# State-space layer of an S5 / sparse-attention decoder: two weight conversions held until the scan ends, the sample group's outputs held until the last states, filler matrix products put behind two steps of the scan

## The chip, the cores and the metric

One core of one Trainium2 chip runs the whole program. The metric is the device time of one execution in microseconds (us); the lower the better. The traces shown are those of one execution taken by the hardware profiler.

## What is computed

Two layers of a decoder run for a prompt group (512 positions) and a sample group (8 sequences of one position each); the weights are shared. The change lies in the first mixer of layer 0, a state-space layer (S5):

```python
x_re = einsum('blgc,gpc->blgp', ug, bb_re)      # inputs into 64 groups of 64 complex states
x_im = einsum('blgc,gpc->blgp', ug, bb_im)
...
_, _, h_re, h_im = lax.associative_scan(complex_affine_combine, (a_re, a_im, x_re, x_im), axis=1)
y = (einsum('blgp,gcp->blgc', h_re, c_re) - einsum('blgp,gcp->blgc', h_im, c_im)) + d_skip * u32
g = gelu(y)
a, b = split(g @ w_glu, 2, axis=-1)
out = a * sigmoid(b)
```

After it come a dense SwiGLU layer, sparse attention, and a mixture of experts, none of which the change touches.

## The kernel before, in words

`build` makes the program; it calls `s5` first, then the GLU loop (lines 283 to 292), the SwiGLU, attention and experts. `s5` cuts the 512 positions into 64 blocks of 8. Its stages are these.

- **Chunks** (lines 565 to 597). For each of eight chunks of eight groups, in the order 0, 4, 1, 5, 2, 6, 3, 7: VectorE (DVE) builds Pm, TensorE (PE) transposes it (L575), ScalarE (ACT) copies the result to Wi (L576), DVE adds a part to `dsk` (L578), PE multiplies Wi with the inputs U (L586), and ACT copies the block sums into the state array XS (L589, four copies a chunk). GpSimd (POOL) builds the output weights Em (L537 to L539) and, in between, the powers Ar, Ai of the transition (L546 to L556).
- **Scan** (lines 611 to 650). `step` does one level of a work-efficient scan over the 64 blocks: products L632 and L633, sums L636 and L638; six levels up, five levels down. DVE does columns 0 to 23 of XS with Ar and Ai held in PSUM (copied there at L607, L608), POOL does columns 24 to 31 by itself (`BLK`). DVE's columns are complete after chunk 6, POOL's only after the last one, chunk 7.
- **Prefetch** (L651). `glu_w(0)` and `glu_w(1)`: each loads 1 MB of GLU weights into a staging tile `wf` (L212; two such slots), ACT makes the f16 high part `wh` (L217) and DVE the f16 rest `wl` from `wf` and `wh` (L218). The loads of blocks 2 and 3 need the staging slots again, so they start when L218 of blocks 0 and 1 are done.
- **Sample group** (lines 659 to 677). POOL computes the sample group's new states (L659 to L665); PE computes its outputs in two halves of 32 pairs of small products (L675, L676), and ACT applies GELU (L677).
- **Prompt outputs** (lines 680 to 711). `toeplitz(b)` (L689) multiplies the inputs with a banded matrix Tp, eight products for each of eight PSUM banks b. Banks for b = 5, 6 and 7 hold Ar, Ai and the scan's scratch until DVE's scan is done; b = 0 to 4 are free earlier. When the scan is done, its states are copied from XS to Hs (L698: the real parts by DVE, the imaginary parts by ACT, two copies each for DVE's columns and two for POOL's), PE adds Hs times Em into the eight banks (L707), and ACT applies GELU (L710).
- **Into the GLU** (lines 715 to 732). PE transposes Y (L719), ACT and DVE split it into f16 parts GH and GL (L725, L726), and the GLU's products begin (L231).

What sets the order: nobody writes the order of an engine's instructions by hand. A planner takes the program in source order and gives each engine, whenever it is free by the planner's own estimate, the ready instruction that stands earliest in the source. So a later instruction is slipped into an earlier sequence wherever that sequence has a gap by the estimate. On the chip each engine then runs its list strictly in that order. `add_manual_dep` adds a wait of one instruction for another, which the planner and the chip both keep.

Of the kernel before, what the change touches and what calls it, by code (L numbers as in the profile page):

```python
# [14 lines left out]
ALU = mybir.AluOpType  # L15
# [4 lines left out]
WS = 256.0  # L20
# [144 lines left out]
def build(tc, a, o, stop=None):  # L165
    nc = tc.nc
    es = ExitStack()
    with es:
        const = es.enter_context(tc.tile_pool(name="const", bufs=1))
        res = es.enter_context(tc.tile_pool(name="res", bufs=1))  # L170
# [35 lines left out]
            else:  # L206
                V.scalar_tensor_tensor(dl, src, scale, dh, op0=ALU.mult, op1=ALU.subtract)

        def wload(src, w, n, pool=wst, tags=("wh", "wl"), parts=1):

            wf = wst.tile([128, w], F32, tag="wf", name=f"wf{n}")
            nc.sync.dma_start(wf, src)  # L212
            wh = pool.tile([128, w], F16, tag=tags[0], name=f"wh{n}")
            wl = pool.tile([128, w], F16, tag=tags[1], name=f"wl{n}")
            for i in range(parts):
                c = slice(i * w // parts, (i + 1) * w // parts)
                S.activation(wh[:, c], wf[:, c], AF.Copy, scale=WS)  # L217
                V.scalar_tensor_tensor(wl[:, c], wf[:, c], WS, wh[:, c], op0=ALU.mult, op1=ALU.subtract)  # L218
            return wh.rearrange("p (k c) -> p k c", c=128), wl.rearrange("p (k c) -> p k c", c=128)

        HV = ((0, 256), (256, NT))
# [39 lines left out]
                for c0, c1 in HV:  # L261
                    S.activation(acc[1][:, c0:c1], act[:, ob, c0:c1], AF.Square)

        def glu_w(ob):
            return wload(a["w_glu"][:, 2 * ob:2 * ob + 2].rearrange("p b k c -> p (b k c)"), 2048, f"g{ob}")

        glu_first = []
        GH, GL = s5(tc, nc, a, o, PS, const, identf, res, wst, lambda: glu_first.extend((glu_w(0), glu_w(1))))
        if stop == "s5":
            nc.sync.dma_start(o["dbg_gh"], GH)  # L270
            nc.sync.dma_start(o["dbg_gl"], GL)
# [75 lines left out]
       }  # L347


def s5(tc, nc, a, o, PS, const, identf, res, wst, prefetch):  # L350
    V, S, G, T = nc.vector, nc.scalar, nc.gpsimd, nc.tensor
    with ExitStack() as es:
        p = es.enter_context(tc.tile_pool(name="s5", bufs=1))
# [211 lines left out]
        for n_, c in enumerate((0, 4, 1, 5, 2, 6, 3, 7)):  # L565
            Pm = wst.tile([128, GC, 8, 16], F32, tag="wh", name=f"Pm{c}")
            prod_v(Pm, pfr, pfs, slice(7, None, -1), 0, b0, b1, c * GC)
            Wi = wst.tile([128, GC, 128], F32, tag="wl", name=f"Wi{c}")
            ic = idc[n_ % 2]
            S.copy(ic[:, :, 128:144], cst[:, c * 8:c * 8 + 8])  # L570
            for j0, nj in ((0, 3), (3, 3), (6, 2)):
                pt = PS(5, 6, 7)
                pv = pt[:, :nj * 144].rearrange("p (g c) -> p g c", c=144)
                for j in range(nj):
                    T.matmul(pv[:, j], Pm[:, j0 + j].rearrange("p k c -> p (k c)"), ic[:, j0 + j], start=True, stop=True)  # L575
                S.copy(Wi[:, j0:j0 + nj], pv[:, :, 0:128])  # L576
                dd = dsk[:, c * 8 + j0:c * 8 + j0 + nj]
                V.tensor_tensor(dd, pv[:, :, 128:144], dd, op=ALU.add)  # L578
            gh = c // 4
            rows = slice(gh * 64, gh * 64 + 64)  # L580
            uq = U[:, c * 8:c * 8 + 8]
            V.tensor_tensor(uq, uq, std.unsqueeze(1).to_broadcast([128, 8, 72]), op=ALU.mult)
            for h in range(2):
                px = PS(5, 6, 7)
                for j in range(4):
                    T.matmul(px[:, j * 72:j * 72 + 72], Wi[:, 4 * h + j, :], U[:, c * 8 + 4 * h + j, :], start=True, stop=True)  # L586
                gp = (c % 4) * 8 + 4 * h
                for ri in range(2):
                    S.copy(XS[rows, 1:73, ri, gp:gp + 4],  # L589
                           px[ri * 64:ri * 64 + 64, :288].rearrange("p (g n) -> p n g", g=4))  # L590
            prod_g(Em[:, c * GC:(c + 1) * GC], pr, pi, slice(1, 9), cst, csw, c * GC)
            if c in (5, 7):
                gs = slice((c - 5) * 8, (c - 5) * 8 + 16)
                for i in range(8):
                    nr_ = 16 * (i + 1)
                    nc.sync.dma_start(Tp[0:nr_, i, :].rearrange("p (h g c) -> p h g c", h=2, c=16)[:, :, gs],
                                      dsk[128 - nr_:128].rearrange("p (h g) c -> p h g c", h=2)[:, :, gs])
# [9 lines left out]
        V.tensor_copy(ArP, Ar[:, :NL])  # L607
        V.tensor_copy(AiP, Ai[:, :NL])  # L608
        m2p = PS(1), PS(2)

        def step(eng, gs, tag, l, tgt0, src0, stride, n):

            w = gs.stop - gs.start
            most = 16 if eng is G else 512 // (2 * w)
            parts = [(i, min(most, n - i)) for i in range(0, n, most)]
            while parts:
                now, parts = parts[:2], parts[2:]
                ops = []
                for k, (i, m) in enumerate(now):
                    def vw(b, r):  # L620
                        b += i * stride
                        return XS[:, b:b + (m - 1) * stride + 1:stride, r, gs]
                    m1 = lt2.tile([128, 16, 2, w], F32, tag=tag, name=f"{tag}a")[:, :m]
                    if eng is G:
                        m2 = lt2.tile([128, 16, 2, w], F32, tag=tag, name=f"{tag}b")[:, :m]
                    else:
                        m2 = m2p[k][:, :m * 2 * w].rearrange("p (n r w) -> p n r w", n=m, r=2)
                    A, B = (ArP, AiP) if eng is V and l < NL else (Ar, Ai)
                    ar = A[:, l:l + 1, gs].unsqueeze(2).to_broadcast([128, m, 2, w])
                    ai = B[:, l:l + 1, :, gs].to_broadcast([128, m, 2, w])  # L630
                    tgt = vw(tgt0, slice(0, 2))
                    eng.tensor_tensor(m1, vw(src0, slice(0, 2)), ar, op=ALU.mult)  # L632
                    eng.tensor_tensor(m2, vw(src0, slice(1, None, -1)), ai, op=ALU.mult)  # L633
                    ops.append((m1, m2, tgt))
                for m1, m2, tgt in ops:
                    eng.tensor_tensor(m2, m1, m2, op=ALU.add)  # L636
                for m1, m2, tgt in ops:
                    eng.tensor_tensor(tgt, tgt, m2, op=ALU.add)  # L638


        BLK = ((V, slice(0, 24), "sv"), (G, slice(24, 32), "sg"))
        for blk in BLK:
            for l in range(6):
                d = 1 << l
                n = 64 // (2 * d)
                step(*blk, l, 2 * d, d, 2 * d, n)
            for l in range(4, -1, -1):
                d = 1 << l
                n = 64 // (2 * d) - 1
                step(*blk, l, 3 * d, 2 * d, 2 * d, n)  # L650
        prefetch()  # L651
        nc.sync.dma_start(o["s5p"].rearrange("r p g -> p r g"), XS[:, 64])

        m1 = late.tile([128, 2, 32, 8], F32, name="hm1")
# [15 lines left out]
        for half in range(2):  # L670
            py = PS(4 + half)
            for j in range(32):
                g = half * 32 + j
                c0 = j * 16
                T.matmul(py[:8, c0:c0 + 16], U[:, g, 64:72], Tp[:, 7, g * 16:g * 16 + 16], start=True, stop=False)  # L675
                T.matmul(py[:8, c0:c0 + 16], h0A[:, g, :], Em[:, g, 0, :], start=False, stop=True)  # L676
            S.activation(ys[:, half * 512:(half + 1) * 512], py[:8], AF.Gelu_apprx_tanh)  # L677

# [12 lines left out]
                             skip_group_check=True)  # L691
        for b in range(4):
            toeplitz(b)
        for (_, gs, _), bs in zip(BLK, ((0, 1, 2, 3, 4, 5), (6, 7))):
            for gh in range(2):
                for ri in range(2):
                    e = S.copy if ri else V.tensor_copy
                    e(Hs[ri * 64:ri * 64 + 64, gh * 32 + gs.start:gh * 32 + gs.stop, :],  # L698
                      XS[gh * 64:gh * 64 + 64, 0:64, ri, gs].rearrange("p n g -> p g n"))
            for b in bs:  # L700
                if b not in pys:
                    toeplitz(b)
                py = pys[b]
                for j in range(4):
                    for gh in range(2):
                        g = gh * 32 + b * 4 + j
                        T.matmul(py[gh * 64:gh * 64 + 64, j * 128:(j + 1) * 128], Hs[:, g, :],  # L707
                                 Em[:, g].rearrange("p i c -> p (i c)"), start=False, stop=(j == 3),
                                 skip_group_check=True)
                S.activation(Y[:, :, 4 * b:4 * b + 4, :].rearrange("p i g c -> p g i c"),  # L710
                             py.rearrange("p (g i c) -> p g i c", g=4, i=8), AF.Gelu_apprx_tanh)
# [1198 lines left out]
```

## Time and profile before

| | us |
|---|---|
| median of 3 runs | 1503.71 (1503.48 to 1504.97) |
| the profiled execution, whole | 1505.52 |
| its span, first instruction to last | 1503.7 |

The profile gives busy times by engine (PE matrix products, PEld their weight loads, DVE, ACT, POOL; SP issues most transfers), the chain of work that ended last, and, by query, instructions in order of time and sums by stretch. A line of the timeline has the start and the length in us, the engine, the source line, what it writes and reads, its shape, how many instructions were merged into the line, and in brackets how long the engine had stood idle and what ended that. The granted clock is given as a share of 2.4 GHz: 1.00 or 0.50 (1.2 GHz), between them for a mixed stretch. PE's instructions overlap, so their pace is read from start to start.

### The profile page before, as it was taken

To read this page: it belongs to the slowest core of one execution; us is meant where nothing else is said; L and a number is where in the kernel's file an instruction comes from. 1 tells how busy PE (TensorE), PEld (TensorE's weight loads), DVE (VectorE), ACT (ScalarE), POOL (GpSimd) and SP (SyncE) were. 2 spreads that over 40 slices of the span, in tenths; PEclk is the share of its full clock that TensorE was granted. 3 is DMA by queue.
4 is the path that set the end of the run, shared out by engine and by line. 5 is a ranking of instruction groups with operands and counts; after the bars stand their busy time and mean duration, and the time that the engine had idled before them with its cause. 6 is when DMAs were issued, how large, how long until landed. Compare 5 with 4: busy or idle time off the path is not lost.

```text
span 1503.7 us, 37358 instructions
## 1 busy us (share of the span) xinstructions
PE 1363.0 (91%) x15585; PEld 1180.1 (78%) x15585; DVE 943.2 (63%) x1641; ACT 771.2 (51%) x1421; POOL 557.4 (37%) x465
## 2 busy tenths in 40 slices
PE   4847999999999999989989979969998999999895
PEld 3836888888888888775777658837877999999884
DVE  8783566232322233594787877475766788878886
ACT  5524344232322112352787777464655776867663
POOL 4991443222222122211122323324830541734935
PEclk9977999999999999999999989968999999999997
DMA  4141742323232333352313221245989999989884
GB/s 167 60 125 58 282 169 78 113 85 112 85 113 73 116 119 139 92 163 100 121 58 99 79 65 31 65 178 199 366 265 331 347 317 380 376 293 391 315 305 147
DMA packets 82049, 262.36 MB, mean 174 GB/s; under 512 B 25242, under 2 KB 40082, under 8 KB 64338
## 3 DMA queue, kind: packets, MB, share of 16 engines
q1 hardware_dynamic: 78770, 249.24, 47.6%
q0 software_dynamic: 2816, 8.52, 1.6%
q8 instruction: 125, 2.05, 0.5%
q10 hardware_dynamic: 288, 2.14, 0.4%
q14 instruction: 50, 0.41, 0.1%
HBM read 232.30 MB, written 21.67 MB: 169 GB/s over the span
## 4 chain that ended last, share of the span: by engine, by line
PE 59%; DVE 14%; DMA 11%; ACT 5%; issue 5%; POOL 4%; SPq 2%; DVEq 0%; ACTq 0%; POOLq 0%
PE ps L231 27%; PE ps L1728 17%; DMA mf<-in_w_mo 3%; DVE ml L1578 2%; PE ps L1076 2%; DMA mf<-in_w_mi 2%; ACT mh L1577 2%; PE ps L1161 2%; DMA yr<-YS,gidxe 2%; PE ps L1676 2%; DMA st<-in_ckc 1%; PE ps L1287 1%; PE ps L1274 1%; DVE tl L205 1%; PE ps L575 1%
## 5 line engine op out<-in xcount | busy, mean ns | idle before, releaser
L1578 DVE SCALAR_TENSOR_TENSOR ml<-mf,mh 128x2048 f16<-128x2048 f32 (+1 forms) x152 | 309.3, 2037 | 77.2 <-ACT mh L1577 74.6
L1728 PEld LDWEIGHTS <-mh 128*128 128x128 f16 x4224 | 328.8, 99 | 14.2 <-ACT mh L1577 2.3
L1577 ACT ACTIVATE mh<-mf 128x2048 f16<-128x2048 f32 (+1 forms) x152 | 256.1, 1685 | 113.5 <-DMA mf<-in_w_mi 34.0
L1728 PE MATMUL ps<-XE,mh 128*128 128x64 f16 (+7 forms) x2816 | 279.9, 230 | 2.8 <-ACT mh L1577 2.1
L1728 PE MATMUL ps<-XE,ml 128*128 128x96 f16 (+7 forms) x1408 | 261.9, 230 | 4.2 <-DVE ml L1578 4.0
L1808 POOL TENSOR_TENSOR AL<-u,AH 128x272 f16<-128x272 f32 (+3 forms) x88 | 171.0, 1947 | 205.0 <-ACT AH L1807 204.0
L1728 PEld LDWEIGHTS <-ml 128*128 128x128 f16 x2112 | 205.3, 99 | 12.2 <-DVE ml L1578 5.9
L231 PEld LDWEIGHTS <-whf 128*128 128x128 f16 x1408 | 137.7, 98 | 18.4
L231 PE MATMUL ps<-GH,whf 128*128 128x256 f16 x704 | 135.7, 274 | 0.0
L231 PE MATMUL ps<-GL,whf 128*128 128x256 f16 x704 | 135.7, 274 | 0.0
L231 PE MATMUL ps<-GH,wlf 128*128 128x256 f16 x704 | 135.5, 274 | 0.0
L1728 PE MATMUL ps<-AL,mh 128*128 128x272 f16 (+7 forms) x704 | 133.7, 230 | 0.9 <-POOL AL L1808 0.9
L1728 PE MATMUL ps<-AH,mh 128*128 128x144 f16 (+7 forms) x704 | 133.1, 230 | 0.0
L1728 PE MATMUL ps<-AH,ml 128*128 128x144 f16 (+7 forms) x704 | 133.0, 229 | 0.0
L320 POOL TENSOR_TENSOR UL<-sf,UH 128x520 f16<-128x520 f32 x22 | 59.4, 2701 | 177.4 <-ACT UH L319 177.4
L317 DVE SCALAR_TENSOR_TENSOR sf<-ps,sf 128x256 f32<-128x256 f32 (+1 forms) x44 | 16.9, 424 | 140.8 <-PE ps L231 140.8
L217 ACT ACTIVATE whf<-wff 128x2048 f16<-128x2048 f32 x22 | 42.0, 1910 | 94.0 <-issue 82.0
L231 PEld LDWEIGHTS <-wlf 128*128 128x128 f16 x704 | 68.9, 98 | 9.3
L231 PEld LDWEIGHTS <-who 128*128 128x128 f16 x704 | 68.9, 98 | 9.2
L1277 DVE CUSTOM_DVE_ANT_0 st<-ps,BB 128x512 f32<-128x512 f32 (+3 forms) x128 | 61.3, 485 | 23.0 <-PE ps L1287 19.8
L1279 ACT ACTIVATE st<-st,mx 128x512 f32<-128x512 f32 (+3 forms) x128 | 71.6, 560 | 5.0 <-DVE mx L1277 4.2
L217 ACT ACTIVATE who<-wfo 128x1408 f16<-128x1408 f32 x16 | 22.0, 1377 | 91.6 <-PE ps L231 77.1
(552 smaller groups left out, 3304.5 us busy)
## 6 DMA issues: line engine op xcount, KB each, us to landing
mf<-in_w_mi SPq DMA_DIRECT2D x88, 1024.0 KB
mf<-in_w_mo SPq DMA_DIRECT2D x64, 704.0 KB
wff<-in_w_fin SPq DMA_DIRECT2D x22, 1024.0 KB
wfo<-in_w_fout SPq DMA_DIRECT2D x16, 704.0 KB
wfg<-in_w_glu SPq DMA_DIRECT2D x8, 1024.0 KB
wfq<-in_w_qk SPq DMA_DIRECT2D x8, 1024.0 KB
HS<-z SPq DMA_DIRECT2D x9, 512.0 KB
st<-in_ckc SPq DMA_DIRECT2D x16, 256.0 KB
```

What stands on the lines that cost most here:

```text
L217: S.activation(wh[:, c], wf[:, c], AF.Copy, scale=WS)
L231: T.matmul(t[:, :c1 - c0], w[:, k0 + k, :], x[k][:, c0:c1] if isinstance(x, list) else x[:, k, c0:c1], start=(first and k == 0 and wi == 0 ...
L320: G.tensor_tensor(UL[:, ob, :], sg, UH[:, ob, :], op=ALU.subtract)
L1076: T.matmul(t[:, :n], w[:, k0 + k], x[:, k, c0:c1], start=(k == 0 and i == 0), stop=(k == 7 and i == 2))
L1161: T.matmul(pv[:n], x[:, k, t0:t1], w, start=(k == 0 and i == 0), stop=(k == 7 and i == 2))
L1277: V.tensor_tensor_reduce(out=st[:, :N], in0=pS[:, :N], in1=bias_cur[0][:, r, 512 - N:], scale=1.0, scalar=3.0e38, op0=ALU.add, op1=ALU.min ...
L1279: S.activation(st[:, :N], st[:, :N], AF.Exp, bias=mx, scale=-1.0, accum_out=st8["sums"][:, 1 + br, r:r + 1])
L1577: S.activation(wh, wf, AF.Copy, scale=WS)
L1578: V.scalar_tensor_tensor(wl, wf, WS, wh, op0=ALU.mult, op1=ALU.subtract)
L1676: T.matmul(px[:, :C0 + C7], hts[tb][:n, k * 128:(k + 1) * 128], OHP[:n, tb], start=(tb == 0), stop=(tb == 4))
L1728: T.matmul(ps, w[:, k0 + k, :], x[:, k, :], start=(k == 0 and i == 0), stop=(k == kn - 1 and i == 2))
L1808: al = G.tensor_tensor(AL[r][:, ob], u, AH[r][:, ob], op=ALU.subtract)
```

## The change

The GLU's first two `wl` conversions (L218) get a wait for DVE's last scan instruction. The first product of each half of the sample group's outputs (L675) gets a wait for the last copy into XS (L589). After `toeplitz(0)` to `toeplitz(3)` in source order stand 12 and 36 new products of 128x512 f16 (the block-0 GLU weights times themselves, into PSUM bank 3, never read); the first 12 wait for DVE's scan level 2 on the way down, the other 36 for level 1. `toeplitz(4)` uses the same bank 3 and now follows them.

```diff
+        def after(x, y):
+            tc.add_manual_dep(x.ins, y.ins.name, mybir.DependencyInfo(
+                mybir.DependencyClass.Sync, mybir.DependencyReason.DATA), reason="order")
...
-                V.scalar_tensor_tensor(wl[:, c], wf[:, c], WS, wh[:, c], op0=ALU.mult, op1=ALU.subtract)
+                t = V.scalar_tensor_tensor(wl[:, c], wf[:, c], WS, wh[:, c], op0=ALU.mult, op1=ALU.subtract)
+                if y is not None:
+                    after(t, y)
...
-        GH, GL = s5(tc, nc, a, o, PS, const, identf, res, wst, lambda: glu_first.extend((glu_w(0), glu_w(1))))
+        GH, GL = s5(tc, nc, a, o, PS, const, identf, res, wst, after,
+                    lambda y: glu_first.extend((glu_w(0, y), glu_w(1, y))) or glu_first[0][0])
...
-                    S.copy(XS[rows, 1:73, ri, gp:gp + 4],
+                    fed = S.copy(XS[rows, 1:73, ri, gp:gp + 4],
...
-                    eng.tensor_tensor(tgt, tgt, m2, op=ALU.add)
+                    done[eng] = eng.tensor_tensor(tgt, tgt, m2, op=ALU.add)
...
+        steps = []
         for blk in BLK:
...
                 step(*blk, l, 3 * d, 2 * d, 2 * d, n)
-        prefetch()
+                if blk[0] is V and l in (2, 1, 0):
+                    steps.append(done[V])
+        whg = prefetch(done[V])
...
-                T.matmul(py[:8, c0:c0 + 16], U[:, g, 64:72], Tp[:, 7, g * 16:g * 16 + 16], start=True, stop=False)
+                t = T.matmul(py[:8, c0:c0 + 16], U[:, g, 64:72], Tp[:, 7, g * 16:g * 16 + 16], start=True, stop=False)
+                if j == 0:
+                    after(t, fed)
...
         for b in range(4):
             toeplitz(b)
+
+        for y, m in zip(steps[:2], (12, 36)):
+            fill = PS(3)
+            for i in range(m):
+                t = T.matmul(fill, whg[:, 4 + i % 4], whg.rearrange("p k c -> p (k c)")[:, 0:512], start=True, stop=True)
+                if i == 0:
+                    after(t, y)
```

## Rows read from the trace of the kernel before

**Rows 1.** The chain that ended last, in order of time: start, length, what.

```profile
77.89 2.63 POOL hm L660
...
85.78 2.78 POOL sga L632
...
125.85 5.34 PE ps L707 x87
```

**Rows 2.** Sums by stretch: PE, PEld, DVE, ACT, POOL busy; granted clock; DMA share; GB/s.

```profile
104.00:118.00 14.00, 0.00 (x0) 0.00 (x0) 12.09 (x26) 0.73 (x1) 11.90 (x25) 0.50 0.02 2
118.00:124.00 6.00, 5.24 (x49) 5.24 (x50) 5.03 (x8) 5.25 (x4) 0.00 (x0) 0.54 0.00 0
124.00:134.00 10.00, 8.21 (x130) 7.73 (x128) 0.00 (x0) 3.37 (x5) 0.00 (x0) 1.00 0.01 2
...
140.00:144.00 4.00, 4.00 (x24) 3.04 (x25) 1.97 (x5) 0.57 (x2) 1.81 (x1) 0.50 0.77 263
```

**Rows 3.** Timeline of POOL around the start of the scan.

```profile
77.22 0.67 POOL L659 TENSOR_TENSOR hm<-h0B,pr 128x256 f32<-128x256 f32 x1
77.80 2.72 POOL L660 TENSOR_TENSOR hm<-h0B,pr 128x256 f32<-128x256 f32 x1
...
81.67 0.63 POOL L556 TENSOR_SCALAR Ai<-Ai 128x160 f32<-128x160 f32 x1
...
85.78 2.78 POOL L632 TENSOR_TENSOR sga<-XS,Ar 128x256 f32<-128x256 f32 x1 [0.45 <-ACT XS L589]
```

**Rows 4.** Timeline of DVE: conversions, ends of scan levels, copies to Hs.

```profile
77.57 2.47 DVE L218 SCALAR_TENSOR_TENSOR wlg<-wfg,whg 128x2048 f16<-128x2048 f32 x1 [1.82 <-ACT whg L217]
...
82.34 0.50 DVE L608 COPY ps<-Ai 128x320 f32<-128x320 f32 x1 [2.09 <-POOL Ai L556]
...
85.70 2.28 DVE L218 SCALAR_TENSOR_TENSOR wlg<-wfg,whg 128x2048 f16<-128x2048 f32 x1
...
105.62 0.50 DVE L638 TENSOR_TENSOR XS<-XS,ps 128x336 f32<-128x336 f32 x1
...
108.81 0.96 DVE L638 TENSOR_TENSOR XS<-XS,ps 128x480 f32<-128x480 f32 x2
...
117.27 1.20 DVE L698 COPY Hs<-XS 64x512 f32<-64x512 f32 x2 [1.74 <-POOL XS L638]
...
119.31 0.77 DVE L638 TENSOR_TENSOR XS<-XS,ps 128x480 f32<-128x480 f32 x2
120.11 3.01 DVE L698 COPY Hs<-XS 64x1536 f32<-64x1536 f32 x2
```

**Rows 5.** Timeline of ACT: second GLU block, last copies to XS, Hs, GELU.

```profile
82.95 1.91 ACT L217 ACTIVATE whg<-wfg 128x2048 f16<-128x2048 f32 x1 [3.27 <-DMA wfg<-in_w_glu]
84.89 0.81 ACT L589 COPY XS<-ps 64x288 f32<-64x288 f32 x2
...
120.11 5.68 ACT L698 COPY Hs<-XS 64x1536 f32<-64x1536 f32 x2 [0.71 <-DVE XS L638]
132.43 4.03 ACT L710 ACTIVATE Y<-ps 128x512 f32<-128x512 f32 x8 [6.63 <-PE ps L689]
```

**Rows 6.** Timeline of PE: sample group, banded products, output products, first GLU products.

```profile
69.72 0.21 PE L675 MATMUL ps<-Tp,U 128*8 128x16 f32 x2
69.78 0.20 PE L676 MATMUL ps<-Em,h0A 128*8 128x16 f32 x2
...
79.73 1.09 PE L689 MATMUL ps<-Tp,U 128*64 128x128 f32 x16 [0.89 <-ACT XS L589]
...
118.77 3.68 PE L689 MATMUL ps<-Tp,U 128*64 128x128 f32 x32 [20.47 <-DVE ps L633]
...
132.18 1.09 PE L707 MATMUL ps<-Em,Hs 128*64 128x128 f32 x13
...
143.54 0.42 PE L231 MATMUL ps<-GH,whg 128*128 128x256 f16 x1
143.75 0.42 PE L231 MATMUL ps<-GL,whg 128*128 128x256 f16 x1
```

More of the change, by code (lines that the diff above doesn't have):

```diff
@@ L207, in hilo, with wload @@
                 V.scalar_tensor_tensor(dl, src, scale, dh, op0=ALU.mult, op1=ALU.subtract)
-        def wload(src, w, n, pool=wst, tags=("wh", "wl"), parts=1):
+        def after(x, y):
+            tc.add_manual_dep(x.ins, y.ins.name, mybir.DependencyInfo(
+                mybir.DependencyClass.Sync, mybir.DependencyReason.DATA), reason="order")
+        def wload(src, w, n, pool=wst, tags=("wh", "wl"), parts=1, y=None):
             wf = wst.tile([128, w], F32, tag="wf", name=f"wf{n}")
@@ L262, in squares, with glu_w @@
                     S.activation(acc[1][:, c0:c1], act[:, ob, c0:c1], AF.Square)
-        def glu_w(ob):
-            return wload(a["w_glu"][:, 2 * ob:2 * ob + 2].rearrange("p b k c -> p (b k c)"), 2048, f"g{ob}")
+        def glu_w(ob, y=None):
+            return wload(a["w_glu"][:, 2 * ob:2 * ob + 2].rearrange("p b k c -> p (b k c)"), 2048, f"g{ob}", y=y)
         glu_first = []
-        GH, GL = s5(tc, nc, a, o, PS, const, identf, res, wst, lambda: glu_first.extend((glu_w(0), glu_w(1))))
+        GH, GL = s5(tc, nc, a, o, PS, const, identf, res, wst, after,
+                    lambda y: glu_first.extend((glu_w(0, y), glu_w(1, y))) or glu_first[0][0])
         if stop == "s5":
@@ L347, with s5 @@
        }
-def s5(tc, nc, a, o, PS, const, identf, res, wst, prefetch):
+def s5(tc, nc, a, o, PS, const, identf, res, wst, after, prefetch):
     V, S, G, T = nc.vector, nc.scalar, nc.gpsimd, nc.tensor
@@ L609, in s5 @@
         m2p = PS(1), PS(2)
+        done = {}
         def step(eng, gs, tag, l, tgt0, src0, stride, n):
```

## The prediction

> **What bounds the kernel now.** I read the chain that ended last first, to see where the changed stage lies on it, then the timelines of the engines it passes through, then the sums by stretch for TensorE's clock. The chain goes through the changed stage on one thread only: POOL's work before the scan, the scan, ACT's copies to Hs, PE's output products [rows 1]. What is saved at the last output product is therefore saved at the end, unless the planner orders a later stage anew. PE is full behind this stage but idle in it: no matmul at all from 104 to 118 us, with the granted clock at 0.50 [rows 2].
>
> Four things in the timelines carry the argument.
> - DVE's scan cannot start before POOL's L556 (81.67 + 0.63 = 82.30), which gives Ai; DVE waits 2.09 us for it [rows 3, 4]. Ahead of L556, L660 took 2.72 us where L659 of the same shape took 0.67 [rows 3]. It ran while DVE's first conversion ran (77.57 to 80.04) [rows 4].
> - The second conversion lies inside the scan: 85.70, 2.28 us [rows 4]. POOL's first scan instruction beside it took 2.78 us [rows 3].
> - In DVE's tail stand the copies of POOL's columns: a wait of 1.74 us for POOL and 1.20 us of copying, before the scan's last level is finished at 119.31 + 0.77 = 120.08 [rows 4].
> - Then DVE copies for 3.01 us and ACT for 5.68 us, to 125.79; PE starts the mass of the output products at 125.85 and ends them at 132.18 + 1.09 = 133.27, which is 7.42 us [rows 1, 4, 5, 6].
>
> **Conversions: what their removal gives.**
> 1. The first one is gone when POOL does L660, so that one should take L659's time: 2.72 - 0.67 = 2.05 us earlier for L556, for L608 and for DVE's scan. The bound below is 0, if L660's length has another reason; I take the whole, since the overlap with the conversion is nearly exact [rows 3, 4].
> 2. The second one leaves the scan: 2.28 us.
> 3. The tail. In source order the copies of DVE's own columns come first; POOL's were slipped in ahead because POOL's columns were ready, by the planner's estimate, shortly before DVE's. DVE's end moves forward by 2.05 + 2.28 = 4.33 us. POOL's moves by the 2.1 us that L632 loses (2.78 to 0.67) and by what its start gains: it waits for the last copy into XS, which stands on ACT behind a conversion that waits 3.27 us for its load [rows 3, 5]. That copy's product on PE needs a DVE instruction that stood behind the first conversion, so it is ready about two us earlier, and the planner should then put the copy ahead of ACT's conversion. DVE thus gains more on the planner's clock than POOL does, and I take it that nothing is slipped in: 1.74 + 1.20 = 2.94 us gone. Bounds: 0 and 2.94.
>
> DVE's scan then ends at 120.08 - 2.05 - 2.28 - 2.94 = 112.8.
>
> **Conversions: what they cost in the new place.** The wait ends with DVE's last scan instruction, exactly when DVE's copies to Hs become ready, and the conversions stand earlier in the source. So I expect DVE to run both first: 2.47 + 2.28 = 4.75 us, to 117.55, with its copies (3.01) behind them, to 120.6. ACT copies from 112.8 to 118.5 [rows 4, 5]. So ACT's copies, which came last before, are replaced by DVE's: the gate for the output products is 120.6 instead of 125.8, **5.2 us** earlier. The bounds: if DVE's copies go ahead of the conversions, the gate is ACT's 118.5 (7.3 us); with nothing gained in the tail it is 123.5 (2.3 us).
>
> Behind the conversions also wait the loads of GLU blocks 2 and 3, since they need the staging slots; SP issues them at about 115 and 118 rather than before the scan. The products of the first GLU blocks are still running at 143.54 [rows 6], so these loads have over 20 us: no cost. SP's next entries are outputs and loads that wait for the scan anyway.
>
> **Sample group.** Its 256 records of products run at two per 0.06 us [rows 6], 7.7 us in all, now behind the last copy into XS, together with banded products of four banks (1.09 us each [rows 6], 4.4 us). Even from 85.7, where that copy ends now [rows 5], this is done by 97.8. PE has nothing else until the fillers, so it costs nothing; with the cover gone it would delay the fillers, which are needed by nobody. What it gives is that the last chunk's products are not cut into; that is part of item 3.
>
> **Fillers.** No row has a 512-column f16 product. The 256-column ones start 0.21 us apart at the 0.50 clock [rows 2, 6], so I estimate 0.42 us at 1.2 GHz and half of that, 0.21, at 2.4. Scan level 2 ends at 105.62 + 0.50 = 106.12 now [rows 4] and, 4.33 earlier, at 101.8; level 1 at 108.81 + 0.96 = 109.77 [rows 4], so 105.4. The clock was low when the banded products began at 118.77 and 1.00 from 124 on [rows 2, 6]: PE had worked some five us. So the first 12 run at the low clock, to 106.8, and 36 at the high one take 7.6 us, to 114.4. Behind them PE has the banded products of banks 4 to 7 (bank 4 now uses the fillers' bank), 4 x 1.09 = 4.4 us at the high clock [rows 6], to 118.8. The gate is 120.6, so the fillers are hidden behind the copies, by 1.8 us; without that cover each costs 0.21 to 0.42. Their gain is small for the same reason: before, the clock was already 1.00 when the mass of the output products began [rows 2], and what ran at the low clock (32 records in 3.68 us against 16 in 1.09 [rows 6]) was waiting for ACT's copies in any case. I take 0; bounds: nothing below, 1.5 us (3.68 - 2 x 1.09) above.
>
> **Output products and after.** Behind the gate PE had one bank's banded products (1.09) besides the output products; that bank now comes earlier, and the two banks of POOL's columns stay behind instead, 32 records at 5.34 us / 87 = 0.061 us [rows 1] less those that ran early: 7.42 us remain. PE ends at 128.0 instead of 133.27. The GELUs, which wait for nearly all of PE's work (6.63 us idle, then 4.03) [rows 5], and the way into the GLU move as a block. So does the low clock at the GLU's start (0.50 over 140 to 144) [rows 2]: no filler stands there.
>
> **Sum.** -5.2 us. The profiled execution took 1505.52 (span 1503.7), 1.81 above the median of the runs; it would become 1500.3. The same difference from the median, 1503.71, gives 1498.5. A measurement of this kernel can tell about 0.2%, 3.0 us, from no change: faster means below 1500.7.
>
> **A rule that speaks against the change.** L660 and L632 show POOL losing about two us beside each conversion [rows 3, 4]. The Trainium skill, "SBUF — State Buffer", section "Who interferes with whom", says that a DVE instruction with two SBUF inputs takes the read port it shares with GpSimd for its whole length, so that a GpSimd instruction that reads SBUF waits; the rows agree. By that rule the conversions can stop POOL in their new place too, if its columns are not done by then (second rival).
>
> **Rivals.**
> - *The slip stays.* The planner again puts POOL's copies into DVE's tail. If POOL ends with DVE, the tail costs 1.20 and a little waiting: gate about 123.5, 2.3 us saved. If the last copy into XS also stays behind ACT's conversion, POOL starts at 85.78 as now and ends 2.1 us earlier than now (117.27), at 115.1; then 1.20 + 1.58 (118.50 to 120.08) + 4.75 + 3.01 give a gate of 125.7: nothing saved. For it: both orders stand so now [rows 4, 5]. Against: DVE gains more than POOL. 1501.4 to 1503.6.
> - *POOL is locked out.* If POOL ends last (115.1 above) and both conversions stop it, it ends by about 119.3; if ACT also has POOL's columns first in its list, as the tail on DVE has now, its copies (1.20 x 5.68 / 3.01 = 2.3 by DVE's ratio) and then 5.68 give a gate of 127.3, 1.5 us later than now: about 1505. Against: it needs three things at once.
> - *Slower: the fillers hold PE.* If the clock does not rise during them, 48 x 0.42 = 20.2 us end at 122.0, the banded products at the low clock (64 x 3.68 / 32 = 7.4) at 129.4, the output products (2 x 7.42) at 144.2: 10.9 us slower, 1514.6. It decides from the point where 101.8 + 48 x 0.21 + n x 0.21 + 4.4 + 7.4 passes 133.27, n = 45 of 48 at the low clock. For it: PE is cold when they start (0.50 over 104 to 118). Against: in the trace the clock rose within five us of the start of the banded products [rows 2, 6].
> - *The lists behind it.* The planner re-orders later stages a little, with either sign; no row prices it.
>
> **How the numbers follow.** Forecast (saves over 3 us; its own range 1494.5 to 1500.5, from the 7.3 us bound with up to 1.5 us from the clock, to just under 0.2%) 0.68; the slip stays 0.14; POOL locked out 0.06; fillers hold PE 0.06; later lists 0.06, of it 0.03 faster, 0.01 same, 0.02 slower. Faster 0.71, same 0.21, slower 0.08. The range goes from 1494.2 to 1503.0: it leaves out the third rival, the second, and the part of the first that saves nothing. The time is the forecast's, 1498.5.
>
> **What would show it.** Right: L660 at some 0.6 us, Ai 2 us earlier, no L218 between scan steps, DVE's last L638 ending near 112.8, then two L218 and the copies on DVE, PE's output products starting near 120.6 and ending near 128, all at 1.00. A step is wrong if POOL's copies still stand before DVE's last L638 (item 3), if the copies precede the conversions (gate 118.5), if fillers still run when Hs is complete (the clock), or if the stage saves five us and the end does not (later lists). The prediction as a whole is wrong if the output products end no earlier than 131.

## The result, and the profile after

The changed kernel takes 1488.53 us (median of 4 runs, 1486.97 to 1490.53) beside 1503.6 for the kernel before (4 runs, 1501.98 to 1504.97): ratio 0.9897, 95% interval 0.9878 to 0.9916, or 15.1 us. A second set of runs (e7 below) gave 0.9923 (0.9902 to 0.9944), 11.6 us. The forecast was 5.2 us, 1498.5 with a range from 1494.2 to 1503.0. The profiled execution after took 1490.53 us, its span 1488.8, with a mean granted clock of 0.957 (0.950 before).

First the timeline of POOL at the start of the scan. L673 is the L660 of [rows 3], L564 its L556, L642 its L632.

```profile
77.78 0.63 POOL L673 TENSOR_TENSOR hm<-h0B,pr 128x256 f32<-128x256 f32 x1
...
79.55 0.63 POOL L564 TENSOR_SCALAR Ai<-Ai 128x160 f32<-128x160 f32 x1
...
80.55 0.71 POOL L642 TENSOR_TENSOR sga<-XS,Ar 128x256 f32<-128x256 f32 x1
```

The two instructions that took 2.72 and 2.78 us beside a conversion take 0.63 and 0.71 with no conversion there. The Trainium skill, "SBUF — State Buffer", section "Who interferes with whom", has a DVE instruction with two SBUF inputs contend with a GpSimd instruction that reads SBUF; with the conversions away the trace agrees again.

The timeline of DVE, to be read against [rows 4]: start of the scan, its tail, the conversions in their new place, the copies to Hs.

```profile
80.21 0.49 DVE L616 COPY ps<-Ai 128x320 f32<-128x320 f32 x1 [6.21 <-POOL Ai L564]
...
111.81 1.22 DVE L720 COPY Hs<-XS 64x512 f32<-64x512 f32 x2 [0.64 <-POOL XS L648]
...
113.76 0.77 DVE L648 TENSOR_TENSOR XS<-XS,ps 128x480 f32<-128x480 f32 x2
114.56 4.49 DVE L223 SCALAR_TENSOR_TENSOR wlg<-wfg,whg 128x2048 f16<-128x2048 f32 x2
118.97 2.99 DVE L720 COPY Hs<-XS 64x1536 f32<-64x1536 f32 x2
```

The scan starts 2.13 us earlier and ends at 114.53 instead of 120.08. POOL's columns are still copied between DVE's last steps. The conversions come first, then the copies, which end at 121.96.

The timeline of ACT, against [rows 5], and that of PE, against [rows 6]:

```profile
114.56 5.89 ACT L720 COPY Hs<-XS 64x1536 f32<-64x1536 f32 x2 [0.57 <-DVE XS L648]
120.48 0.60 ACT L732 ACTIVATE Y<-ps 128x512 f32<-128x512 f32 x1
123.20 0.60 ACT L732 ACTIVATE Y<-ps 128x512 f32<-128x512 f32 x1 [2.12 <-PE ps L729]
...
127.57 1.09 ACT L732 ACTIVATE Y<-ps 128x512 f32<-128x512 f32 x2 [0.28 <-PE ps L729]
```

```profile
101.71 13.50 PE L713 MATMUL ps<-whg 128*128 128x512 f16 x48 [10.28 <-DVE XS L648]
115.14 2.89 PE L704 MATMUL ps<-Tp,U 128*64 128x128 f32 x48
117.81 1.09 PE L729 MATMUL ps<-Em,Hs 128*64 128x128 f32 x16
118.69 1.09 PE L704 MATMUL ps<-Tp,U 128*64 128x128 f32 x16
...
122.10 5.86 PE L729 MATMUL ps<-Em,Hs 128*64 128x128 f32 x92 [0.23 <-DVE Hs L720]
127.90 3.33 PE L741 MATMUL ps<-identf,Y 64*128 64x64 f32 x64
```

Of the kernel before, PE's timeline at the same place, the eighth bank's banded products (in part) and the first transposes:

```profile
131.30 0.76 PE L689 MATMUL ps<-Tp,U 128*64 128x128 f32 x10
...
135.04 3.21 PE L719 MATMUL ps<-identf,Y 64*128 64x64 f32 x48 [1.77 <-ACT Y L710]
```

The last output product ends at 127.96, 5.3 us earlier than before. But the GELUs no longer stand in one block of 4.03 us behind 6.63 us of waiting: each follows its own bank, and the transposes (L741) start with no gap, where before they began 1.77 us behind the last output product. All banded products (L704) stand ahead of the mass of the output products; before, those of the eighth bank ran among the last.

The sums by stretch (columns as in [rows 2]):

```profile
100.00:105.00 5.00, 3.29 (x8) 1.20 (x9) 4.90 (x12) 0.00 (x0) 4.44 (x10) 0.50 0.00 0
105.00:110.00 5.00, 4.94 (x18) 1.93 (x17) 5.00 (x10) 0.00 (x0) 4.62 (x7) 0.75 0.00 0
110.00:115.00 5.00, 5.00 (x25) 2.16 (x22) 4.27 (x11) 2.59 (x3) 1.62 (x3) 1.00 0.00 0
...
140.00:144.00 4.00, 4.00 (x38) 3.52 (x37) 0.43 (x2) 2.60 (x5) 0.00 (x0) 1.00 0.06 20
```

The clock rises under the fillers and is still 1.00 at 140 to 144 us, where it was 0.50 before. To follow this through all runs I use one landmark: the start of the 501st product of the gated layer, in a stretch where PE is full. It stands at 197.68 us before and at 187.29 after, 10.4 us earlier: 5.3 from the output products, 1.8 from the gap ahead of the transposes, and 3.3 in what follows, where the clock was low before.

### The profile page after: what moved, and what is told of

It is laid out like the page before. It is cut to its first block, busy times and chain, and to the rows that moved or that the text cites. A ratio compares the mean times of both kernels' runs of the same rounds, so it can differ in the third digit from the quotient of the medians.

```text
span 1488.8 us, 37460 instructions
## 1 busy us (share of the span) xinstructions
PE 1364.2 (92%) x15633; PEld 1174.0 (79%) x15633; DVE 940.7 (63%) x1641; ACT 772.6 (52%) x1421; POOL 548.8 (37%) x465
## 3 DMA queue, kind: packets, MB, share of 16 engines
q8 instruction: 125, 2.05, 0.6%
## 4 chain that ended last, share of the span: by engine, by line
PE 57%; DVE 11%; DMA 10%; POOL 8%; issue 6%; ACT 6%; SPq 2%; DVEq 0%; POOLq 0%; ACTq 0%
PE ps L238 28%; PE ps L1750 16%; DMA mf<-in_w_mi 3%; DMA mf<-in_w_mo 3%; PE ps L1098 2%; DVE ml L1600 2%; PE ps L1309 2%; PE ps L1698 2%; ACT mh L1599 2%; PE ps L1183 1%; DMA st<-in_ckc 1%; PE ps L1296 1%; POOL Em L547 1%; POOL tg L546 1%; POOL Em L545 1%
## 5 line engine op out<-in xcount | busy, mean ns | idle before, releaser
L1750 PE MATMUL ps<-AH,mh 128*128 128x144 f16 (+7 forms) x704 | 133.3, 230 | 2.2 <-ACT mh L1599 2.2
L1750 PE MATMUL ps<-AH,ml 128*128 128x144 f16 (+7 forms) x704 | 133.3, 230 | 1.3 <-DVE ml L1600 1.3
L1309 PE MATMUL ps<-identf,st 128*128 128x128 f32 x320 | 60.4, 288 | 11.1 <-DVE tl L205 9.1
```

The source lines that it names most:

```text
L1309: T.transpose(pT[:, kb * 128:(kb + 1) * 128], st[:, kb * 128:(kb + 1) * 128], identf)
L1750: T.matmul(ps, w[:, k0 + k, :], x[:, k, :], start=(k == 0 and i == 0), stop=(k == kn - 1 and i == 2))
```

## The experiments

Two theories for what went beyond the forecast. **Order**: the wait makes DVE's copies late, the planner therefore puts all banded products ahead of the output products, and the GELUs overlap. **Clock**: the fillers hold the clock up. A third, **lists**: later stages fell out better. The table holds all runs.

| kernel | ratio to before (95%) | last output product ends | 501st gated product | clock under 0.9 at 132 to 144 us |
|---|---|---|---|---|
| before, first profile | 1 | 133.3 | 197.68 | yes |
| before, second profile (e8) | - | 132.7 | 194.26 | no |
| changed, first profile | 0.9897 (0.9878 to 0.9916) | 128.0 | 187.29 | no |
| changed, second (e7) | 0.9923 (0.9902 to 0.9944) | 127.4 | 186.73 | no |
| e1 conversions only | 0.9931 (0.9905 to 0.9956) | 127.1 | 188.98 | yes |
| e2 sample group only | 1.0006 (0.9983 to 1.0029) | 132.8 | 198.74 | yes |
| e3 fillers only | 0.9987 (0.9970 to 1.0004) | 134.1 | 198.51 | yes |
| e4 no fillers | 0.9946 (0.9928 to 0.9963) | 127.5 | 187.71 | no |
| e5 order alone | 0.9977 (0.9964 to 0.9990) | 132.4 | 191.37 | no |
| e6 order undone | 0.9968 (0.9955 to 0.9980) | 129.2 | 190.65 | no |
| e9 conversions behind | 0.9958 (0.9942 to 0.9973) | 128.7 | 194.43 | yes |
| e10 behind, ordered | 0.9908 (0.9891 to 0.9926) | 127.3 | 186.31 | no |
| e11 shared copies | 0.9906 (0.9887 to 0.9924) | 125.5 | 184.49 | no |
| e12 the same, no fillers | 0.9900 (0.9882 to 0.9918) | 125.7 | 184.76 | no |

**The parts by themselves: e1, e2, e3, e4.**

Taking out the conversions' wait (e2, e3), the sample group's (e1, e3) and the fillers (e1, e2, e4) are these three edits of the changed kernel:

```diff
-        whg = prefetch(done[V])
+        whg = prefetch(None)
...
-                if j == 0:
-                    after(t, fed)
...
-        for y, m in zip(steps[:2], (12, 36)):
-            fill = PS(3)
-            for i in range(m):
-                t = T.matmul(fill, whg[:, 4 + i % 4], whg.rearrange("p k c -> p (k c)")[:, 0:512], start=True, stop=True)
-                if i == 0:
-                    after(t, y)
```

> Of the three edits only the wait of the two weight conversions for the scan is kept; the sample group's products stand early again and there is no filler. Theory clock (the fillers keep TensorE at 1.00 through the output products, transposes and the start of the gated layer, and that is what went beyond the forecast): the scan still ends near 114.5 us and the output products near 128, but the granted clock is 0.50 somewhere between 128 and 136 us, the transposes take 4.5 us or more, and the whole gains 8 to 11 us (1493 to 1496). Theory order (the wait makes the copies of the states late on VectorE, so all banded products stand ahead of the output products and the GELUs overlap them): transposes begin near 128 without a gap, the clock is of no weight, the whole gains 13 to 15 us (1489 to 1491).

> Of the three edits only the sample group's wait for the last states is kept; the conversions stand in the scan as before, no filler. Theory clock: no change beyond 1 us (1502.5 to 1504.5), the clock at 140 to 144 us stays 0.50. Theory order: the same, since the banded product of the eighth bank still stands among the output products; 1502.5 to 1504.5. A rival, that taking 128 small products and their GELUs out of the stretch before the scan frees ScalarE for the last copies of the states, would bring the scan's end down by 1 us or more and show it alone.

> Of the three edits only the 48 filler products are kept, behind the same steps of the scan; the conversions and the sample group stand as before. Theory clock: the scan ends where it did (120.1) and the output products near 133.3, but the granted clock at 140 to 144 us is 1.00 and not 0.50, and the whole gains 3 to 5 us (1498.5 to 1500.5). Theory order: no change beyond 1 us (1502.5 to 1504.5), and the GELUs still stand in one block behind the eighth bank's banded product.

> The change without its fillers: both waits are kept. Theory clock: 3 to 5 us of the gain go (1491.5 to 1493.5), the granted clock is 0.50 in the stretch of the transposes or the first products of the gated layer (128 to 136 us), which begins 3 us later than in the changed kernel. Theory order: 1488 to 1490, the first dense product of the gated layer starts near 132 us as in the changed kernel. A third reading, that about 5 us came from lists of the later layers that fell out better by luck, would show a shift that is the same as the changed kernel's up to 150 us and differs behind 220 us.

The conversions' wait alone gives most of the gain: 10.4 us by the ratio, of the 11.6 to 15.1 of the whole change. The sample group's alone gives nothing that can be told, and neither do the fillers alone (the intervals hold 1). In e3, ACT's timeline has the one block of GELUs (first line), and the sums by stretch have the clock low behind it in spite of the fillers (second line); in e4, without them, the sums by stretch show the clock low under the banded products and at 1.00 in the gated layer.

```profile
133.28 4.03 ACT L730 ACTIVATE Y<-ps 128x512 f32<-128x512 f32 x8 [8.16 <-PE ps L702]
```

```profile
140.00:144.00 4.00, 4.00 (x24) 3.02 (x23) 2.82 (x6) 1.36 (x4) 1.80 (x1) 0.50 0.61 204
```

```profile
115.00:120.00 5.00, 5.00 (x54) 5.00 (x52) 5.00 (x3) 4.98 (x2) 0.00 (x0) 0.54 0.44 143
...
140.00:144.00 4.00, 4.00 (x38) 3.53 (x37) 0.76 (x2) 1.09 (x1) 0.14 (x1) 1.00 0.19 45
```

So the fillers by themselves do not hold the clock up behind the block. In e1 the clock theory's number (8 to 11 us; 10.4 by the ratio) was met, and the clock did fall there, but the transposes took 3.45 us and followed without a gap, as the order theory had it:

```profile
127.02 3.45 PE L733 MATMUL ps<-identf,Y 64*128 64x64 f32 x64
```

```profile
132.00:136.00 4.00, 4.00 (x24) 2.88 (x24) 1.39 (x4) 1.50 (x2) 1.80 (x1) 0.57 0.97 369
```

What the fillers are worth together with the two waits stays open. The ratio of e4 (8.1 us) lies below what either theory expected, and below the changed kernel's: by 3.5 us against e7, where the intervals overlap, and by 7.4 against the first set, where they don't. At the landmark e4 is only 0.4 and 1.0 us behind the changed kernel's two profiles, but its profile is of the shortest of its twelve executions (1491.02 beside a median of 1498.31).

**Order alone, on the kernel before (e5), and order undone, on the changed one (e6).**

In e5 each bank's first output product waits for the last banded product:

```diff
-        for b in range(4):
-            toeplitz(b)
+        for b in range(8):
+            last = toeplitz(b)
...
+                        if j == 0:
+                            after(t, last)
```

In e6 the eighth bank's banded products wait for the sixth bank's last output product:

```diff
-                    toeplitz(b)
+                    toeplitz(b, last[5] if b == 7 else None)
```

> The kernel before with one edit that the change does not contain: all eight banks' banded products are put ahead of the first output product by a dependency; conversions, sample group and scan stay as before, no filler. Theory order: the scan ends at 120.1 us and the last output product near 133.3 us as before, but the GELUs run one by one beside the products instead of in one block from 132.4 us, the transposes start within 0.5 us of the last output product instead of 1.8 us behind it, and the granted clock does not fall to 0.50 at 140 to 144 us: the dense products of the gated layer stand 4 to 5.5 us earlier at 150 us (no scan gain at all), and the run is 0.2 to 0.4% faster. If the gain beyond the forecast hung on the earlier scan or on the conversions instead, this kernel shows no change: within 1 us at 150 us.

> The changed kernel with one edit: the eighth bank's banded product is held behind the output products of the first six banks, where it stood before the change; both waits and the fillers stay. Theory order: the GELUs stand in one block behind that banded product again, the last output product still ends near 128 us, the transposes begin 1.5 us or more behind it, the clock falls to 0.50 for some us at the start of the gated layer, and the shift against the kernel before at 150 us is 5 to 6.5 us, not 10.4. Theory clock (fillers): the fillers hold 1.00 all the same, and the shift at 150 us stays above 9 us.

ACT and PE in e5: the scan and the copies end at 119.4 and 125.1 (the second profile of before, below, has 119.5 and 125.3), yet the GELUs follow the products and the transposes have no gap.

```profile
131.55 0.60 ACT L718 ACTIVATE Y<-ps 128x512 f32<-128x512 f32 x1 [0.28 <-PE ps L713]
132.42 0.60 ACT L718 ACTIVATE Y<-ps 128x512 f32<-128x512 f32 x1 [0.28 <-PE ps L713]
```

```profile
125.18 7.20 PE L713 MATMUL ps<-Em,Hs 128*64 128x128 f32 x122 [1.10 <-ACT Hs L704]
132.32 3.07 PE L727 MATMUL ps<-identf,Y 64*128 64x64 f32 x64
```

ACT and PE in e6: the block is back behind the banded product that was moved, and so is the gap of 1.77 us.

```profile
128.35 4.03 ACT L734 ACTIVATE Y<-ps 128x512 f32<-128x512 f32 x8 [8.05 <-PE ps L704]
```

```profile
130.96 3.63 PE L743 MATMUL ps<-identf,Y 64*128 64x64 f32 x64 [1.77 <-ACT Y L734]
```

At the landmark e5 stands 6.3 us ahead of the first profile of before (4 to 5.5 expected) and 2.9 ahead of the second; e6 7.0 ahead of the first (5 to 6.5 expected), 3.9 behind the changed kernel's second.

Order is a cause, both ways. Alone it is worth 0.23% (3.5 us; 1.5 to 5.4 by the interval). Taken out of the changed kernel it costs the step from 0.9923 to 0.9968, 6.8 us, of which 3.9 show at the landmark, and what is left is 4.8 us, near the 5.2 that I had forecast for the whole change. One thing the order theory got wrong: the clock stayed at 1.00 in e6 although the block was there.

The built instruction lists show how the block arises. Of the kernel before, the end of PE's list and the GELUs in ACT's (place in the list, line, operation, what it waits for):

```
198 L707 MATMUL ps_1154<-Em,Hs 64x128
199 L689 MATMUL ps_1172<-Tp,U 64x128 x8
200 L707 MATMUL ps_1172<-Em,Hs 64x128 x8
...
95 L710 ACTIVATE Y<-ps_1038 128x4x8x16 [waits PE_49]
96 L710 ACTIVATE Y<-ps_1047 128x4x8x16
...
102 L710 ACTIVATE Y<-ps_1172 128x4x8x16 [waits PE_49]
```

Seven GELUs share the first one's wait, which the trace ends with the banded product L689; in the changed kernel and in e5 each of the eight has a wait of its own. The shared wait stood in every kernel whose eighth banded product lies among the last output products. Why the program is built so was not looked into.

**The two kernels once more: e7 and e8**, unchanged.

> The changed kernel once more, on the chip of these runs. Theory order with scatter behind it (only the 10.4 us up to the gated layer belong to the change; the other 4.9 us of the first profile are the difference of two single runs): ratio 0.992 to 0.995, and a shift at 150 us of 10.4 us again with another curve behind 220 us. Theory of better lists in the later layers: ratio 0.989 to 0.991 and the same curve as the first time, 12.7 us at 254 to 610 us and 15.9 us at 690 to 800 us.

> The kernel before once more, for a second profile of it. If the later part of the first profile is one draw among several, the same products of this profile stand within 0.5 us of it up to 220 us and wander by 2 to 5 us behind that, with nothing changed; if the later part repeats itself, they stay within 1 us throughout.

The changed kernel repeats 10 to 11 us at the landmark (186.73), but its later curve differs: measured against the first profile of before, the shift over 400 to 600 us is 11.0 us where it was 12.7, and at 1300 us 8.9 where it was 13.8. The kernel before differs from itself by nearly as much: its second profile stands 3.2 us ahead of its first over 400 to 600 us and 6.9 over 800 to 1000. That second profile has the same block of GELUs (first line), and the clock does not fall behind it (second line): 2.9 us come from that alone, between the transposes' start (0.5 us earlier) and the landmark (3.4).

```profile
131.89 4.03 ACT L710 ACTIVATE Y<-ps 128x512 f32<-128x512 f32 x8 [6.63 <-PE ps L689]
```

```profile
140.00:144.00 4.00, 4.00 (x38) 3.47 (x36) 1.43 (x4) 0.00 (x0) 0.94 (x1) 1.00 0.85 356
```

Against this profile the changed kernel's second gains 7.5 us at the landmark instead of 11.0, and its first 7.0 instead of 10.4. The 4.6 us that the first pair of profiles showed behind the landmark (15.0 at the end of the spans) did not come again: the changed kernel's second profile ends 9.1 us ahead. So single profiles don't decide the theory of lists.

It is not excluded either, because the later order did change. In the traces the order of ACT's instructions behind 210 us differs between the kernel before and the changed one in 52 places, up to 934 us, and DVE's in 59, up to 1020 us. In e5 it differs from the kernel before in 3 and 1, none behind 256 us, and in e2 in none. The four kernels that share the changed kernel's later order but for a few places (changed, e9, e10, e11) gain 2.7 to 4.8 us more by their ratios than at the landmark, taken against the mean of the two profiles of before; for e2 and e5 that difference is 1.9 and -1.1, for the kernels with still other later orders -0.5 to 4.5. By this estimate the later order may be worth some us. Each of these differences is uncertain by about 3 us, and no run has the later order as its only difference, so it is not shown. The later order also differs between e6 and the changed kernel, and between e4 and it (52 and 67 places on ACT): the part of their differences that lies behind the landmark may be its doing too.

My expectation that the two profiles of before would agree within 0.5 us up to 220 us was wrong for the same reason, the clock.

**The conversions behind DVE's copies: e9, e10; the copies shared anew: e11, e12.**

In e9 the conversions to the low halves are issued later, each behind hv, DVE's last copy of its own columns:

```diff
-        whg = prefetch(done[V])
+        lows = []
+        whg = prefetch(lows)
...
+            while lows:
+                lows.pop(0)(hv)
```

e10 adds the dependency of e5; e11 adds to e10 another sharing of the copies, and e12 is e11 without the filler loop:

```diff
-                    e = S.copy if ri else V.tensor_copy
+                    e = (S.copy if ri else G.tensor_copy) if gs.start else (S.copy if ri and gh else V.tensor_copy)
```

> The changed kernel with the two conversions put behind VectorE's copies of the last states instead of ahead of them; the filler products stay. By the queue alone the copies on VectorE end 4.5 us sooner, ScalarE's copies (to 120.4 us) open the output products, and the kernel gains 1.5 us over the changed one: 11.5 to 12.5 us at 150 us against the kernel before. Theory order says the opposite: in the built kernel the eighth bank's banded product stands among the last output products again and the GELUs in one block, so the 3.9 us that the order was worth are lost and the 1.5 us won: 7.5 to 9 us at 150 us, ratio 0.994 to 0.996.

> The same, with all eight banded products ahead of the output products by a dependency. Theory order: both gains stand, the GELUs run one by one, the last output product ends near 126.5 us, 11.5 to 13 us at 150 us, ratio 0.991 to 0.993. If the order had no weight, it is as the kernel with the conversions behind and without the dependency, within 1 us.

> The same again, with the eight copies of the last states shared anew: GpSimd takes the two of its own columns that VectorE took between its last scan steps, VectorE takes three of the four large ones and ScalarE one. By rows of the changed kernel VectorE's scan ends 1.9 us sooner (112.7), its three copies of 1.5 us at 117.2, ScalarE's one behind two small ones at 116.9: the output products open near 117.2 to 118 us instead of 121.96, their last ends near 123 to 124 us, 14 to 15.5 us at 150 us, ratio 0.989 to 0.991. Against it: GpSimd's copies may be kept waiting by VectorE's and end behind them; then the gain over the kernel with only the dependency is under 1 us.

> The kernel with the shared copies, without the filler products. At 0.50 the 48 banded products behind the scan take 5.4 us (rows of the kernels without fillers) and not 2.9: if the scan ends at 112.7 us they end at 118.1, about 1 us behind the copies. So the fillers are worth 0.5 to 1.5 us here if they count at all; if the clock theory held in full, 3 us or more, with 0.50 at the start of the gated layer.

e9 is the sharpest test: the copies end at 120.1 instead of 121.96, so by the queues it should win. The planner puts the eighth banded product back among the last output products, ACT shows the block, and the clock falls:

```profile
127.81 4.03 ACT L742 ACTIVATE Y<-ps 128x512 f32<-128x512 f32 x8 [7.73 <-PE ps L710]
```

```profile
132.00:136.00 4.00, 4.00 (x50) 3.88 (x49) 3.50 (x6) 3.53 (x8) 0.00 (x0) 0.50 0.00 0
136.00:140.00 4.00, 4.00 (x22) 2.95 (x22) 1.60 (x4) 0.52 (x2) 1.80 (x1) 0.50 0.80 268
```

Its shift at the landmark is 3.3 us, under the 7.5 to 9 expected. The clock accounts for that: from the last output product to the landmark e9 needs 65.8 us, and e6, with the same block and the clock at 1.00, 61.5. The ratio, 0.9958, is where it was expected. With the dependency (e10) it is 0.9908, and the transposes follow without a gap:

```profile
120.13 7.20 PE L742 MATMUL ps<-Em,Hs 128*64 128x128 f32 x126 [2.44 <-ACT Hs L729]
127.26 3.06 PE L756 MATMUL ps<-identf,Y 64*128 64x64 f32 x64
```

The order is thus worth 7.5 us here, the low clock included, and it is the lateness of DVE's copies that made the planner choose it. e10's last output product ends at 127.3 (126.5 expected), and at the landmark e10 is 11.4 us ahead of the first profile of before (11.5 to 13 expected). It shows little more than the changed kernel, though its copies end 1.3 us earlier than in e7: all but 2 of its 128 records of output products stand behind ACT's last copy, while in the changed kernel 36 run ahead of the last copy. Both at once were not tried.

In e11, DVE, POOL and PE (one timeline each):

```profile
111.85 0.77 DVE L653 TENSOR_TENSOR XS<-XS,ps 128x480 f32<-128x480 f32 x2
112.65 5.54 DVE L729 COPY Hs<-XS 64x1536 f32<-64x1536 f32 x3
```

```profile
111.94 3.35 POOL L729 COPY Hs<-XS 64x512 f32<-64x512 f32 x2
```

```profile
118.33 7.17 PE L742 MATMUL ps<-Em,Hs 128*64 128x128 f32 x126 [0.40 <-DVE Hs L729]
```

With nothing slipped into its tail, DVE's scan ends at 112.62. The output products end at 125.5, 1.8 us ahead of e10 and 2.5 ahead of the changed kernel's first profile. That is later than the 123 to 124 expected, since DVE's copies end at 118.19 and not at 117.2 (the last section has the reason). The whole time can't tell these gains: 0.9906 and, without fillers, 0.9900, beside 0.9897 and 0.9923. In e12 the banded products run at the low clock (0.50 over 110 to 115) and still end at 116.9, ahead of the last copy at 118.35:

```profile
111.54 5.39 PE L710 MATMUL ps<-Tp,U 128*64 128x128 f32 x48 [18.37 <-DVE ps L648]
116.72 1.21 PE L736 MATMUL ps<-Em,Hs 128*64 128x128 f32 x6
118.50 7.17 PE L736 MATMUL ps<-Em,Hs 128*64 128x128 f32 x122 [0.57 <-DVE Hs L723]
```

The fillers are worth 0.3 us at the landmark there, under the 0.5 to 1.5 expected, and nothing in the ratio.

## Why the prediction was wrong in size

1. **POOL's release** (2.05 us): right, 2.13 measured.
2. **The conversion out of the scan** (2.28): right; together with POOL's release and 1.1 us less waiting in the tail the scan ends 5.55 us earlier.
3. **The tail** ("I take it that nothing is slipped in", 2.94): wrong. The copies stand there still; only the wait fell, from 1.74 to 0.64. The premise, that DVE gains more than POOL, did not hold on the chip: POOL began its scan at 80.55 instead of 85.78 and ended it 5.45 us earlier, while DVE stood ready for the copies only 4.36 us earlier. The scan ended at 114.53, not 112.8. The price was right: in e11, with the slip gone, it ends at 112.62.
4. **The gate** (conversions first, copies to 120.6): right in order, 121.96 by item 3.
5. **The end of the output products** (128.0): 127.96, by two errors that cancel. The gate came 1.36 us late, and 5.9 us of products stood behind it instead of 7.42. The eighth bank's banded products ran ahead of the gate as forecast; but 36 records of output products also did, 26 of them of POOL's two banks, which I had left mostly behind. That the forecast end came out to 0.04 us was luck.
6. **"The GELUs ... and the way into the GLU move as a block. So does the low clock at the GLU's start"**: this is the step that failed. I read the 6.63 us in [rows 5] as a wait for nearly all of PE's work and did not ask which product ended it. The row names it: PE's L689, a banded product that needs no state. My own working had this product done at 118.8, ahead of the gate, and kept the wait for it all the same. Once DVE's copies are late the planner puts it first, and the wait goes. That is worth 3.5 us alone (e5) and 7.5 us on the kernel with the conversions behind the copies (e9 against e10); e6 against e7 gives 6.8 us, 3.9 of them by the landmark. The low clock was no fixed cost either: the second profile of the kernel before doesn't have it.
7. **The fillers**: no gain taken. None can be told by themselves (e3) or with the shared copies (e11 against e12); in the changed kernel itself a gain of some us is not excluded (e4). They ended at 115.2 where I had 114.4 and held up nothing.

With item 6 undone the change gains 4.8 us against 5.2 forecast. What the medians show beyond the landmark's 7 to 11 us, up to 15.1, stays open. The rival of lists behind the stage, which I gave 0.03 on the faster side and priced by no row, is still possible there, and single profiles of one kernel wander by up to 5.5 us in the later stages.

## What to carry to other kernels

When a block of work waits, ask which instruction releases it and whether that one could run earlier; here the releaser was named in the row and depended on nothing that was late. A wait added in one queue changes a list planner's order in others, also in stages far behind it, so look at the new lists, and hold an order that pays with a dependency of its own rather than leave it to a side effect. Before a difference behind the changed stage is explained, take a second profile of the unchanged kernel.

## What the hardware showed that was not expected

The same kernel, with the same gap on PE, has TensorE's clock at 0.50 over 140 to 144 us in one execution and at 1.00 in another, for 2.9 us. Over the fourteen profiles it was low near the start of the gated layer in four of the six with the block of GELUs, with fillers (e3, e9) or without, and in one of the eight without the block (e1). With the fillers and no block it was low in none of four (the changed kernel twice, e10, e11). So few profiles don't settle what decides it.

POOL's copies beside DVE's cost DVE time: three copies of 64x1536 took 5.54 us in e11, while two took 2.99 with POOL idle, so 1.05 us more than three times the mean of those. One by one the three took 1.68, 2.32 and 1.48 us, the last with POOL done; POOL's two took 1.05 and 2.25. POOL's second ended 0.95 us behind the end of DVE's first, and DVE's second 1.38 us behind the end of POOL's second: each took about its own length after the other had ended. The Trainium skill, "SBUF — State Buffer", section "Who interferes with whom", says that a DVE copy that uses both port pairs and a GpSimd instruction keep each other out for a whole instruction; these times fit that, and no row shows which ports a copy used.
